# The pace of attention beside the projections: 27 and 26 k steps a head in place of 25, in a hybrid SSD and attention block

## The chip, the core and the metric

The kernel runs on one core of a Trainium2 chip. The core's engines follow streams of their own: TensorE (PE in the profile, its weight loads as PEld), VectorE (DVE), ScalarE (ACT), GpSimd (POOL) and SyncE (SP), which here only issues DMAs. The metric is the time of one execution on the device in microseconds, as the median of several runs.

## The reference, cut to what matters

A block for 512 tokens with 2048 features. One input projection feeds two mixers, a state-space mixer and an attention with three branches; both go through an output projection, and a gated feed-forward follows.

```python
def reference(x, ...):
    u = rmsnorm(x, attn_norm_w)
    z, xbc, dt_raw, q, kc, vc, ks, vs, kw, vw, gate_raw = split(u @ w_in)
    y_ssd = ssd_mixer(z, xbc, dt_raw, ...)
    y_att = nsa_mixer(q, kc, vc, ks, vs, kw, vw, gate_raw, ...)
    h = x + concatenate([y_ssd, y_att]) @ w_out
    v = rmsnorm(h, ffn_norm_w)
    h = h + (silu(v @ w_gate) * (v @ w_up)) @ w_down
    return rmsnorm(h, final_norm_w)

# nsa_mixer: 16 heads of 64, in 4 groups that share keys and values
    p_cmp = softmax(mask(q k_cmp / 8))          # 31 compressed keys
    o_sel = softmax(mask(q_rot ks / 8)) vs      # selected blocks: at 512 tokens all causal ones
    o_win = softmax(mask(q_rot kw / 8)) vw      # a window of 512: again all causal ones
    o = g0 * o_cmp + g1 * o_sel + g2 * o_win
```

## The kernel before, in words

**Number format.** Every large product is done as three matmuls of a high and a low half: high by high, high by low, low by high. ScalarE makes the high half of an operand (`a_hi`, L124), VectorE the low half (`lo`, L127).

**Projection tiles.** The input projection is 41 tiles of 128 output rows (`Unit`), the output projection 16 more. A tile goes through 16 k steps (output tiles 11, 12 or 8); each k step is the three matmuls L234, L235, L236 and then one `sch.tick()`. Weights arrive in sub-tiles of four k steps; `issue_split` forms their halves three sub-tiles ahead (`whi`, `wlo`). After a tile its evacuation runs as a generator (`ev_q`, `ev_ks`, `ev_vs`, `ev_z`, `ev_os`).

**The scheduler in the code.** `Sched` holds generators. A generator emits instructions and then yields a number of ticks to be left alone. `run_until(flags)` ticks, without matmuls of a tile, until the flags are set. `run_unit` (L217) calls it before each tile: L224 asks that the evacuation of the tile two before has ended.

**The tiles beside attention.** In the order they run (L1008 to L1012): Z4, VS1, KS1, Q1a, Q1b, Z5, Z6, Z7, VS2, KS2, Q2a, Q2b, VS3, KS3, Q3a, Q3b, then the 16 output tiles; 256 and 186 k steps. From Z4 on PE's instructions stand in the order in which they are written; the other engines' order is set by the planner of the language. Keys (KS), values (VS) and queries (Q) of group g are made by the tiles that carry its number. Their buffers are two deep: `ev_vs` and `ev_ks` of group g wait, after a few ticks, for the flag ("a", g - 2), set when all of group g - 2 is done (L720, L760). `ev_q` waits in the same way for heads before it.

**Attention.** `attention()` (L811) goes through 112 items: 4 groups, 4 heads, 7 items a head. At step s it emits the scores of item s (`score`: two matmuls, a mask and a minimum on VectorE, the exponential on ScalarE), yields one tick, transposes item s - 3 (`trans`: into one of two banks ps_t, whose halves pth and ptl ScalarE and VectorE read out) and scales item s (`norm`), yields PACE ticks, and for the last item of a branch emits the product with the values (`pvmm`, L919). So a head takes 7 + 18 = 25 ticks. At the start of group g it waits for the keys and the first queries of the group; the first product of a group waits for the values and the compressed branch (`compressed`).

**The join to the feed-forward.** Ahead of the last output tile (8 k steps), `pre_last` (L1054) waits for the end of attention and for the evacuation of the tile before, closes attention's buffers, and opens the feed-forward's in their place. What is left of the output projection (L1231 to L1233) follows the last tile; its weights come from `Z<-in_w_out`, its halves are `R`.

Of the kernel before, what the change touches and what calls it, by code (L numbers as in the profile page):

```python
# [26 lines left out]

NS = [11, 11] + [12] * 13 + [8]
KSUB = 4
PACE = [3, 2, 3, 2, 3, 2, 3]  # L30
LAG = 3
EB = 5
LEAD = 3
# [81 lines left out]
def body(ctx, tc, xT, w_in, w_out, w_gate, w_up, w_down, w1k, w1v, cols, rows, kst, out):  # L115
# [695 lines left out]
    def attention():  # L811
# [48 lines left out]
        def score(g, h, br, i):  # L860
            L = 128 * (i + 1)
            q = R["rq", g, h // 2][:, h % 2, i * 128:(i + 1) * 128]
            p = ps_s()
            o = p[:, 0:L] if i else p[:, 0:256].rearrange("p (b k) -> p b k", b=2)
            for n, t in enumerate(R["k", g]):
                pe.matmul(o, q, t[:, br, 0:L] if i else t[:, :, 0:128], start=(n == 0), stop=(n == 1))
            e = ap.tile([128, 512], F32, tag="e", name="e", bufs=EB)
            m = ap.tile([128, 8], F32, tag="em", name="em", bufs=EB + 1)
            pr[g, h, br, i] = (e, m)
            for b, c, m in sides(br, i, m):  # L870
                dve.tensor_tensor_reduce(e[:, c], p[:, c], kcs(K_AM + 512 - L, L), -0.125, 3e38,
                                         ALU.add, ALU.min, m[:, 0:1])
                act.activation(e[:, c], e[:, c], AF.Exp, scale=-1.0, bias=m[:, 0:1], accum_out=m[:, 1:2])
# [6 lines left out]
        def norm(g, h, br, i):  # L880
            e, m = pr[g, h, br, i]
            for b, c, m in sides(br, i, m):
                gc = (4 * g + h) * 3 + 1 + b
                dve.reciprocal(m[:, 2:3], m[:, 1:2])
                if b:
                    dve.tensor_scalar(e[:, c], e[:, c], m[:, 2:3], gat[:, i, gc:gc + 1],
                                      op0=ALU.mult, op1=ALU.mult)
                else:
                    mul(dve, m[:, 3:4], m[:, 2:3], gat[:, i, gc:gc + 1])
                    a_hi(e[:, c], e[:, c], scale=m[:, 3:4])  # L890

        def trans(g, h, br, i):
            e, m = pr.pop((g, h, br, i))
            if (br, i) in ((0, 1), (2, 0)):
                pt[g, h, br // 2] = (ap.tile([128, 13, 128], F32R, tag="pth", name="pth", bufs=2),
                                     ap.tile([128, 13, 128], F32R, tag="ptl", name="ptl", bufs=2))
            p = ps_t()
            for kb in range(i + 1 if i else 2):
                pe.transpose(p[:, kb * 128:(kb + 1) * 128], e[:, kb * 128:(kb + 1) * 128], ident)
            for b, c, _ in sides(br, i, m):  # L900
                th, tl = pt[g, h, b]
                s = p[:, c].rearrange("p (a b) -> p a b", b=128)
                d = slice(i, 3 * i + i + 1, 3)
                a_hi(th[:, d, :], s)
                lo(dve, tl[:, d, :], s, th[:, d, :])

        def pvmm(g, h, br):
            th, tl = pt.pop((g, h, br))
            if br == 0:
                ch, cl = R["cc", g]  # L910
                o = po[h] = ps_v()
                pe.matmul(o, vpad[:, h, :], ch, start=True, stop=False)
                pe.matmul(o, vpad[:, h, :], cl, start=False, stop=False)
            o = po[h]
            v = R["v", g]
            for kb in range(4):
                for t in (th, tl):
                    rhs = t[:, 4 * kb:3 * kb + 4, :].rearrange("p a b -> p (a b)")
                    pe.matmul(o[:, kb * 128:512], v[:, kb, br, :], rhs, start=False,  # L919
                              stop=(br == 1 and kb == 3 and t is tl))  # L920
            if br == 1:
                if h % 2 == 0:
                    R["at"] = ap.tile([128, 512], F32, tag="at", name="at", bufs=1)
                at = R["at"]
                a, b = (0, 64) if h % 2 == 0 else (64, 0)
                fo = ap.tile([128, 512], F32, tag="fo", name="fo", bufs=1)
                act.activation(fo[a:a + 64, :], o[b:b + 64, :], AF.Copy)
                add(dve, at[a:a + 64, :], o[a:a + 64, :], fo[a:a + 64, :])
                if h % 2:
                    k = 2 * g + h // 2  # L930
                    if "ma" in P2:
                        h_, l_ = P2["ma"][k]
                        a_hi(h_, at)
                        lo(dve, l_, at, h_)
                    else:
                        parts(at_d[k], at)
                        P2["at"] = k
                    sch.flags.add(("at", k))
# [5 lines left out]
        for s in range(n + LAG + 1):  # L944
            if s < n:
                g, h, br, i = items[s]
                if (h, br, i) == (0, 0, 1):
                    yield from sch.wait(("k", g), ("q", g, 0))
                if (h, br, i) == (2, 0, 1):
                    yield from sch.wait(("q", g, 1))  # L950
                if (h, br, i) == (2, 0, 2) and g < 3:
                    sch.add(compressed(g + 1))
                score(*items[s])
                if (br, i) == (1, 3):
                    sch.flags.add(("h", g, h))
            yield 1
            if 0 <= s - LAG < n:
                trans(*items[s - LAG])
            if s < n:
                norm(*items[s])  # L960
            yield PACE[s % len(PACE)]
            if 0 <= s - LAG - 1 < n and items[s - LAG - 1][2:] in ((2, 0), (1, 3)):
                g, h, br, _ = items[s - LAG - 1]
                br %= 2
                if (h, br) == (0, 0):
                    yield from sch.wait(("v", g), ("cc", g))
                pvmm(g, h, br)
                sch.flags.add(("pv", g, h, br))
                if (h, br) == (3, 1):
                    sch.flags.add(("a", g))  # L970
# [652 lines left out]
    def g_rhs(p, lo_):  # L1623
        a = G_POS[V_OF[p]]
        return lambda k: (G[lo_ + k][:, a, 0, :], G[lo_ + k][:, a, 1, :])
# [155 lines left out]
    def down_before(v, n):  # L1781
        def before():
            if n == 1:
                assert v < NJ - 2 or not any(fz.busy[NZ2:])
                add_h(v)
                if v:
                    P2["A2"] = P2["A"][:, 70:76, :]
            elif n == 0 and v == 27:
                x = GRING * 2 + 1
                assert max(i for i, y in enumerate(visits) if y[1] <= x < y[2]) < v  # L1790
                close_pool("t0")
                P2["X"] = open_pool("t0", side="right").tile([128, 32, 128], F32, name="X")
            elif (v, n) == (0, 0):
                close_pool("E")
                P2["E2"] = P2["E"] = open_pool("E").tile([128, NE, 128], F32, name="E2")
        return before
# [13 lines left out]
    for v, (j, a, b) in enumerate(visits):  # L1810
# [14 lines left out]
        for n, p in enumerate(SEQ_D):  # L1825
            blk, sums = q["form"][p]
            if n == 0 and v in (2, 3):
                later[5 + (v == 3)] = len(items)
            s = Step(blk, g_rhs(p, a), bk(p), after=af(p),
                     before=down_before(v, n) if n < 2 else None, sums=sums)  # L1830
# [70 lines left out]
    sch.add(ssd_core())  # L1901
    sch.add(compress())
    sch.add(attention())
    for n, u in enumerate(units[:n_att]):
        if n == 4:
# [97 lines left out]
```

## Time and profile before

| | |
|---|---|
| median of the runs | 2195.72 us (2189.53 to 2196.98, 3 runs) |
| profiled execution | 2193.74 us, span 2192.0 us |
| PE busy | 98% of the span |
| VectorE / ScalarE / GpSimd busy | 81% / 55% / 20% |
| scores of attention, first to last product | 346.8 to 781.5 us |
| last output tile ends | 796.6 us |

The page gives busy time as shares of the span. Where idle time ends at another engine's work, the line names what was waited for, as in `[1.48 <-DVE sc L133]`: idle 1.48 us, ended by VectorE's instruction of line 133 that wrote sc. Matmuls overlap in a pipeline: the duration of one is longer than the distance from its start to the next one's.

### The profile page before, as it was taken

What the parts mean: (1) busy time and instruction counts of PE and PEld (TensorE: products, weight loads), DVE (VectorE), ACT (ScalarE), POOL (GpSimd) and SP (SyncE); (2) the same over time, 40 slices, a digit from 0 to 9 for tenths busy, and PEclk for the clock granted to TensorE, in tenths of its full rate; (3) what the DMA queues carried; (4) which work ended last, traced back from release to release, by engine and by line L of the source; (5) the groups of instructions that cost most, each with busy time, mean ns of one, the idle gap of its engine ahead of it and who ended that gap; (6) DMA issues with size and microseconds to landing.
All of it is one profiled execution on the core that took longest, in us unless ns stands there. A gap on an engine that the chain in (4) does not pass through costs nothing. (4 is left out here: it accounts for less than half of the span.)

```text
span 2192.0 us, 35313 instructions
## 1 busy us (share of the span) xinstructions
PE 2143.6 (98%) x12828; PEld 1891.6 (86%) x12828; DVE 1773.5 (81%) x2799; ACT 1210.5 (55%) x2022; POOL 433.8 (20%) x444
## 2 busy tenths in 40 slices
PE   8999999999999999999999999999999899999997
PEld 6888887888788887888888888888888899999897
DVE  6799767878896658888888888888888888887786
ACT  5465456676676657565555555555555443443353
POOL 0002224424431134000001000000000231222232
PEclk9999999999999999999999999999999999999999
DMA  5222342223464476878888788888878879897973
GB/s 202 92 70 71 127 145 91 72 97 103 144 216 119 108 223 204 252 211 253 229 239 246 218 252 222 245 242 221 254 215 269 292 195 318 239 286 201 320 189 107
DMA packets 179182, 427.17 MB, mean 195 GB/s; under 512 B 20624, under 2 KB 27808, under 8 KB 179008
## 3 DMA queue, kind: packets, MB, share of 16 engines
q1 hardware_dynamic: 139760, 321.66, 43.6%
q0 software_dynamic: 29584, 85.90, 20.1%
q10 hardware_dynamic: 9664, 17.36, 2.2%
q8 instruction: 101, 1.65, 0.3%
q14 instruction: 73, 0.60, 0.1%
HBM read 358.78 MB, written 62.39 MB: 192 GB/s over the span
## 5 line engine op out<-in xcount | busy, mean ns | idle before, releaser
L124 ACT ACTIVATE R<-Z 128x1024 fp32r<-128x1024 f32 (+4 forms) x446 | 406.8, 925 | 395.7 <-DVE Z L136 308.1
L127 DVE TENSOR_TENSOR R<-Z,R 128x1024 fp32r<-128x1024 f32 (+4 forms) x355 | 376.5, 1068 | 39.1 <-issue 13.8
L234 PE MATMUL ps_g<-u,whi 128*128 128x512 f32 x778 | 318.7, 410 | 2.1 <-ACT whi L124 2.1
L236 PE MATMUL ps_g<-u,wlo 128*128 128x512 f32 x778 | 306.7, 394 | 1.0 <-DVE wlo L127 0.8
L235 PE MATMUL ps_g<-u,whi 128*128 128x512 f32 x778 | 305.4, 393 | 0.0
L1227 PE MATMUL ps_s<-u,R 128*128 128x512 f32 (+1 forms) x1160 | 251.5, 347 | 0.6 <-ACT A L1436 0.6
L1227 PEld LDWEIGHTS ps_s<-u,R 128*128 128x128 f32 x1160 | 188.6, 188 | 28.4 <-ACT A L1436 1.2
L127 DVE TENSOR_TENSOR wlo<-wraw,whi 128x512 fp32r<-128x512 f32 x211 | 160.1, 761 | 63.6 <-ACT whi L124 59.9
L124 ACT ACTIVATE whi<-wraw 128x512 fp32r<-128x512 f32 x211 | 131.5, 626 | 112.3 <-PE ps_g L235 80.2
L236 PEld LDWEIGHTS ps_g<-u,wlo 128*128 128x128 f32 x778 | 146.4, 188 | 33.9 <-DVE wlo L127 2.3
L234 PEld LDWEIGHTS ps_g<-u,whi 128*128 128x128 f32 x778 | 146.8, 189 | 24.7 <-ACT whi L124 2.4
L235 PEld LDWEIGHTS ps_g<-u,whi 128*128 128x128 f32 x778 | 147.2, 189 | 22.6
L1227 PE MATMUL ps_t<-u,R 128*128 128x512 f32 (+1 forms) x600 | 131.4, 347 | 0.0
L1227 PE MATMUL ps_g<-u,R 128*128 128x512 f32 x584 | 131.3, 349 | 0.0
L1227 PE MATMUL ps_g<-T,R 128*128 128x512 f32 (+1 forms) x584 | 127.2, 350 | 0.0
L1227 PE MATMUL ps_s<-T,R 128*128 128x512 f32 (+1 forms) x560 | 125.5, 349 | 0.0
L1227 PE MATMUL ps_s<-V,R 128*128 128x512 f32 (+1 forms) x568 | 123.4, 348 | 0.0
L127 DVE TENSOR_TENSOR E<-Z,R 128x1024 fp32r<-128x1024 f32 (+1 forms) x91 | 111.5, 1226 | 4.4 <-PE ps_t L1227 3.8
L136 DVE TENSOR_TENSOR Z<-Z 128x1024 f32<-128x1024 f32 (+4 forms) x99 | 107.1, 1081 | 8.3 <-POOL Z L136 6.4
L1227 PEld LDWEIGHTS ps_t<-u,R 128*128 128x128 f32 x600 | 98.0, 188 | 14.0
L136 DVE TENSOR_TENSOR A<-ps_g,A 128x512 f32<-128x512 f32 (+1 forms) x102 | 67.3, 664 | 51.5 <-PE ps_g L1227 39.1
L1227 PEld LDWEIGHTS ps_g<-u,R 128*128 128x128 f32 x584 | 95.9, 188 | 13.9
(504 smaller groups left out, 5542.8 us busy)
## 6 DMA issues: line engine op xcount, KB each, us to landing
Z<-in_w_up SPq DMA_DIRECT2D x94, 512.0 KB, 4.6
Z<-in_w_gate SPq DMA_DIRECT2D x94, 512.0 KB, 5.5
wraw<-in_w_in SPq DMA_DIRECT2D x164, 256.0 KB, 2.6
g_d<-A SPq DMA_DIRECT2D x147, 256.0 KB, 6.3
Z<-in_w_up POOLq DMA_DIRECT2D x37, 512.0 KB, 7.5
Z<-in_w_gate POOLq DMA_DIRECT2D x37, 512.0 KB, 7.4
u<-g_d SPq DMA_DIRECT2D x70, 256.0 KB, 5.5
Z<-in_w_down SPq DMA_DIRECT2D x55, 320.0 KB, 4.7
```

The source lines that it names most:

```text
L124: act.activation(dst, src, AF.Copy, scale=scale)
L127: eng.tensor_tensor(dst, src, f(hi), ALU.subtract)
L136: eng.tensor_tensor(o, a, b, ALU.add)
L234: pe.matmul(p, hi_t[i][:, j, :], ah, start=(k == 0), stop=False)
L235: pe.matmul(p, hi_t[i][:, j, :], al, start=False, stop=False)
L236: pe.matmul(p, lo_t[i][:, j, :], ah, start=False, stop=(k == u.nk - 1))
L1227: pe.matmul(o, w, x, start=start, stop=(k == n - 1 and o is q), skip_group_check=not fresh[0])
```

## The change

The list of seven PACE values becomes four lists, one for each group. In the first three groups they add up to 20 a head, with the 7 single ticks 27 k steps; in the last group to 19, that is 26.

```diff
-PACE = [3, 2, 3, 2, 3, 2, 3]
+PACE = [[3, 3, 3, 3, 3, 2, 3]] * 3 + [[3, 3, 3, 2, 3, 2, 3]]
...
-            yield PACE[s % len(PACE)]
+            yield PACE[min(s // 28, 3)][s % 7]
```

No instruction is added or removed; they stand at other places among the matmuls of the tiles.

## The prediction

> **What bounds the kernel now.** I read the page's head first, then the windows of the stretch in which attention runs, then the waits of PE alone in it, and last the order of time at the places named. The page says that PE is the engine to follow:
>
> ```profile
> span 2192.0 us, 35313 instructions
> PE 2143.6 (98%) x12828; PEld 1891.6 (86%) x12828; DVE 1773.5 (81%) x2799; ACT 1210.5 (55%) x2022; POOL 433.8 (20%) x444
> ```
>
> All PE work that the change touches stays the same work; it is only dealt out in another order. So the time can move only by PE's idle time and by a lower clock. The windows show where these are. The cut at 584.60 us is the end of the projection tile KS3, the cut at 344.80 the start of Z4 (k step 0 below), and 781.50 is the last matmul of attention. Columns are the window, its length, then PE, PEld, DVE, ACT, POOL busy with counts, the granted clock and DMA.
>
> ```profile
> 344.80:584.60 239.80, 231.25 (x1190) 192.17 (x1189) 196.87 (x508) 166.40 (x381) 87.23 (x93) 0.99 0.30 98
> 584.60:781.50 196.90, 196.57 (x1010) 164.57 (x1009) 138.88 (x389) 125.31 (x301) 47.26 (x58) 1.00 0.50 147
> ```
>
> Of PE's idle time beside attention 239.80 - 231.25 = 8.55 us lie before 584.6, and only 0.33 us after it, at the same pace of 25. The waits of PE in the first window:
>
> ```profile
> PE ps_t L899 <- DVE ptl L127: 3.4, 4, 1.4
> PE ps_g L234 <- ACT whi L124: 2.1, 1, 2.1
> PE ps_t L843 <- DVE sc L133: 1.5, 1, 1.5
> PE ps_g L236 <- DVE wlo L127: 0.8, 2, 0.5
> PE ps_v L919 <- DVE ptl L127: 0.4, 1, 0.4
> ```
>
> They are waits for VectorE and ScalarE: a transpose that finds both ps_t banks unread, a weight half not yet formed. The sum of the rows is 8.2 us.
>
> **Counting the change.** The code deals work by ticks: one k step of a tile (three matmuls, L234 to L236) is one tick, and attention advances by 1 + PACE ticks per score item, seven items a head. I count from k step 0. Attention first waits for the compressed branch until tick 36, six ticks late. The last product of group 1 comes at the end of s = 59, so after 60 items: eight heads of 25 and four items of 4, 3, 4, 3, with the 6 ticks and the one at the start 200 + 14 + 7 = tick 221. The last of group 3 comes after 116 items: 400 + 14 + 7 = tick 421 (k step 420; one tick falls in the gap before the second output tile). The trace agrees: k steps (L235) and score matmuls (L866, two per item) in the same windows are
>
> ```profile
> 344.80:584.60 239.80, 88.46 (x225) 42.84 (x225) 0.99 0.30 98
> 584.60:781.50 196.90, 76.80 (x196) 37.04 (x196) 1.00 0.50 147
> 344.80:584.60 239.80, 30.86 (x122) 21.67 (x122) 0.99 0.30 98
> 584.60:781.50 196.90, 26.04 (x102) 18.14 (x102) 1.00 0.50 147
> ```
>
> 224 to 225 k steps with 61 items, then 196 with 51: 420 and 112. Twenty-two k steps (781.5 to 796.6) then run with no attention beside them.
>
> After the change, the same count gives: the first wait is four ticks, group 1 ends at 8 x 27 + 4 x 4 + 5 = tick 237, group 3 at 12 x 27 + 4 x 26 + 15 + 5 = tick 448. Now the limit at L224: a tile starts only when the tile two before it has been read out and its evacuation has ended. The evacuation of VS3 (ended k step 208) holds at L720 until group 1 is done, because the buffers of v are two. The first q tile of group 3, two tiles after it, starts at k step 224. Before, group 1 was done at 221, three ticks early. After, it is done at 237: the loop of L224 then ticks 13 times **without a matmul of the tile between**. Attention is pushed through these 13 ticks dry, so it catches up: it stands at item 60 at k step 224 (before: item 60 at 221). From there 27 and 26 a head end it at k step 434 instead of 420. That is exactly where the last output tile is opened (L1055), so nothing more is waited for there: 8 k steps run after it in place of 22. So the change has three parts.
>
> *Part 1, k steps 0 to 224: attention slower.* Fewer items share the same stretch, 57 for 61. Nothing is removed. What is gained is at most the idle time there, 8.55 us, and the clock that one of these waits costs:
>
> ```profile
> 370.41 0.63 PE L843 MATMUL ps_t<-ident,sc 128*128 128x128 f32 x4 [1.48 <-DVE sc L133]
> 372.45 0.66 PE L899 MATMUL ps_t<-ident,e 128*128 128x128 f32 x2 [0.73 <-DVE ptl L127]
> 373.34 0.63 PE L235 MATMUL ps_g<-u,whi 128*128 128x512 f32 x1
> 373.77 0.63 PE L236 MATMUL ps_g<-u,wlo 128*128 128x512 f32 x1
> ...
> 783.65 0.39 PE L234 MATMUL ps_g<-u,whi 128*128 128x512 f32 x1
> 783.88 0.39 PE L235 MATMUL ps_g<-u,whi 128*128 128x512 f32 x1
> 784.10 0.39 PE L236 MATMUL ps_g<-u,wlo 128*128 128x512 f32 x1
> 784.33 0.39 PE L234 MATMUL ps_g<-u,whi 128*128 128x512 f32 x1
> ```
>
> ```profile
> 372.00:374.00 2.00, 1.54 (x5) 1.38 (x6) 1.90 (x8) 0.87 (x3) 0.00 (x0) 0.55 0.37 119
> 374.00:376.00 2.00, 2.00 (x6) 1.55 (x6) 0.70 (x2) 1.03 (x2) 0.00 (x0) 0.59 0.03 12
> ```
>
> A k step takes 784.33 - 783.65 = 0.68 us at full clock. At a clock of 0.55 to 0.59 a matmul came every 0.43 us in place of 0.23; over six of them that is 1.2 us. Bounds of the gain: 0 and 8.55 + 1.2 = 9.8 us. The value: a transpose waits for a bank read two items earlier; two items are now 2 x 27/7 k steps apart in place of 2 x 25/7, 0.57 k step or 0.39 us more; three items (the lag from a score to its transpose) are 0.59 us more. The four waits of L899 shorten by 0.39 each (1.56), the one for whi by 0.59, those for wlo and L919 (0.8 and 0.4, shorter than 0.59 each time) go. The one of L843 is left, since its chain counts ticks from the q tile, not items. I take 1.56 + 0.59 + 0.8 + 0.4 = 3.4 us gained.
>
> *Part 2, the 13 dry ticks at k step 224.* They hold 13 x 7/27 = 3.4 items. What an item costs VectorE and ScalarE, from the undisturbed stretch 660 to 781 us with 34 scores:
>
> ```profile
> L127 DVE TENSOR_TENSOR ptl<-ps_t,pth 128x384 fp32r<-128x384 f32 (+3 forms) x39 | 19.1, 490 | 6.2 <-ACT pth L124 5.7
> L871 DVE CUSTOM_DVE_ANT_0 e<-ps_s,kc 128x384 f32<-128x384 f32 (+3 forms) x34 | 16.6, 497 | 14.3 <-PE ps_s L866 14.2
> L886 DVE TENSOR_SCALAR e<-e,em,gat 128x256 f32<-128x256 f32 (+3 forms) x19 | 8.6, 452 | 0.6
> L884 DVE RECIPROCAL em<-em 128x1 f32<-128x1 f32 x35 | 5.7, 163 | 9.1 <-ACT e L873 8.6
> L871 DVE DVE_READ_ACCUMULATOR2_ANT em<- 128x1 f32 x34 | 2.8, 83 | 0.0
> L133 DVE TENSOR_TENSOR em<-em,gat 128x1 f32<-128x1 f32 x16 | 2.5, 157 | 0.4
> ```
>
> That is 55.3 us over 34, 1.63 us of VectorE an item. PE needs, from the second window, (196.57 - 196 x 0.68) / 51 = 1.24 us an item. So in the dry stretch VectorE has 3.4 x 1.63 = 5.5 us to do while PE has 4.2 us, where otherwise each item has 27/7 x 0.68 = 2.6 us of k steps beside it. Idle of PE: at least 0 (what VectorE has left can be done behind the next k steps, whose weight halves are formed three sub-tiles ahead), 1.3 us by these sums, and more by what else stands in VectorE's order at that place, the evacuation of KS3 and the two parts of v:
>
> ```profile
> 585.25 0.68 DVE L133 TENSOR_TENSOR kt<-ps_g,rrow 128x512 f32<-128x512 f32 x1
> 588.06 0.69 DVE L133 TENSOR_TENSOR ro<-kt,kc 128x512 f32<-128x512 f32 x1
> 586.92 0.75 DVE L594 SCALAR_TENSOR_TENSOR lp<-gy,colc,hp 128x512 fp32r<-128x512 f32 x1 [0.98 <-ACT hp L124]
> 583.59 0.42 DVE L127 TENSOR_TENSOR v<-ps_m,v 128x256 fp32r<-128x256 f32 x1
> ```
>
> With all of it (0.68 + 0.69 + 0.75 + 2 x 0.42 = 3.0) the idle is 4.3 us. If it is spread as at 370 us, the clock falls for 1.2 us more: upper bound 5.5 us. I take 2.0 us, near the sum without the evacuations, since KS3's read-out and v are not waited for by an item of the stretch.
>
> The Trainium skill, "TensorE: Matmul & The Clock Gate", section "HAM oscillation", says that the clock halves only after idle gaps beyond about 3.4 us; by that rule 2 us of idle in pieces cost no clock, and a whole dry gap of 4.3 us would cost an estimated 1.7 us of it. The trace differs: 1.48 and 0.73 us of idle within 4 us sufficed at 370 us.
>
> *Part 3, the end.* Groups 2 and 3 run at 27 and 26; with 0.33 us of idle there is nothing to gain. Attention's last matmul now stands 8 k steps (5.5 us) ahead of the first output remainder (L1231) in place of 15.1 us. Before, the order there was:
>
> ```profile
> 777.52 1.91 SPq L1166 DMA_DIRECT2D Z<-in_w_out  x4
> 781.41 0.27 PE L919 MATMUL ps_v<-ptl,v 128*128 128x128 f32 x1
> 784.60 0.69 DVE L127 TENSOR_TENSOR u<-at,u 128x512 fp32r<-128x512 f32 x1 [0.31 <-ACT u L124]
> 786.53 1.90 ACT L124 ACTIVATE R<-Z 128x640 fp32r<-128x640 f32 x3 [0.23 <-issue]
> 788.78 0.69 DVE L127 TENSOR_TENSOR E<-Z,R 128x512 fp32r<-128x512 f32 x1
> 796.57 0.39 PE L1231 MATMUL ps_g<-u,R 128*128 128x512 f32 x1
> ```
>
> The last attention rows u take 785.3 - 781.5 = 3.8 us behind it: within 5.5. The first forms R (1.9 us of ScalarE for three, to 789.5 us with VectorE's) came 8.0 us behind it; if they hang on attention's buffers, they are 8.0 - 5.5 = 2.5 us late. If not, nothing: the loads that feed them were issued from 777.5 us on, ahead of attention's end, so I take 0 and keep 2.5. The DMA issues, on SP's and ScalarE's queues, are the same in number and order.
>
> **Sum.** -3.4 + 2.0 + 0 = -1.4 us. The profiled execution took 2193.74 us, 1.98 below the median 2195.72. So 2192.3 for such an execution and 2194.3 as a median: no change that can be told, since some 0.3% (6.6 us) is what a measurement of this kernel separates from none.
>
> **The rivals.**
> - *The early waits vanish.* All 8.55 + 1.2 us go and the dry stretch costs its 2.0: -7.8, a median of 2187.9. For it: the second window, with fewer items of evacuation, has no wait at all, so the waits may be a threshold. Against: VectorE is busy 196.87 of 239.80 us (82%) there, and 4 items fewer x 1.63 us take 6.5 us of it, 3 points.
> - *The dry stretch decides (slower).* PE runs 13 ticks with nothing to cover VectorE, the evacuations stand in front, the clock falls, and the early waits stay, because they come from the order on VectorE and ScalarE and not from load: +5.5, 2201.2. It decides from the point at which the stretch's idle exceeds the gain of part 1. For it: three parts of idle already tripped the clock once. Against: four items are 4.2 us of PE work.
> - *The end.* The forms are late by 2.5 us: -1.4 + 2.5 = +1.1, 2196.8. Against: the early loads.
> - That the change does nothing is excluded by the counts, except that the dry ticks give most of the slowing back by k step 224.
>
> **How the numbers follow.** The forecast 0.52, the early waits 0.14, the dry stretch 0.22, the end 0.12. The runs of the kernel before went from 2189.53 to 2196.98, so each case has some 4 us about it. Faster by over 0.3%: most of the second case and a little of the first, 0.16. Slower by over 0.3%: two fifths of the dry stretch, which alone is +0.25%, with a little of the end and of the forecast, 0.14. Within: 0.70. The range takes in both outer cases with about 2 us beyond: 2186 to 2203; the forecast's own is 2190 to 2199.
>
> **What would show it.** In the profile after: the number of k steps up to the last L919 of attention is 434 and not 420; between two k steps near 585 us stand some four scores, three sets of transposes and two products with no L234 between; idle of PE there near 2 us; the waits at L899 before it fall from 3.4 us to under 2; no wait at L1231 at the join. It is wrong if the dry stretch is not there, if the early waits stay whole, or if PE waits for forms at the join.

## The result and the profile after

The changed kernel takes 2204.73 us (median of 7 runs, 2201.68 to 2207.55), the kernel before in the same comparison 2195.46 us (7 runs): a ratio of 1.0051, 95% interval 1.0041 to 1.006. It is slower, by 9.3 us between the medians, and 1.7 us above the predicted range. The profiled execution took 2203.51 us. Head of the page after:

```profile
span 2201.7 us, 35334 instructions
PE 2146.3 (97%) x12828; PEld 1894.0 (86%) x12828; DVE 1779.5 (81%) x2799; ACT 1209.4 (55%) x2022; POOL 430.6 (20%) x444
```

The counts of these rows are those of before (the 21 more in all are semaphore instructions), the span is 9.7 us longer. The windows of the kernel after, cut where the predicted pieces meet: k step 0, the stretch without k steps, the end of attention, the end of the last output tile (window, length, PE, PEld, DVE, ACT, POOL busy with counts, clock, DMA):

```profile
344.20:582.00 237.80, 225.73 (x1153) 187.41 (x1152) 194.63 (x479) 158.69 (x358) 86.64 (x94) 0.99 0.31 99
582.00:593.40 11.40, 7.79 (x37) 6.36 (x35) 9.70 (x30) 8.05 (x20) 7.39 (x11) 0.71 0.32 102
593.40:799.60 206.20, 206.20 (x1056) 173.16 (x1055) 140.59 (x391) 127.08 (x308) 41.40 (x51) 1.00 0.50 143
799.60:805.20 5.60, 5.60 (x28) 4.63 (x27) 2.21 (x3) 1.96 (x3) 1.33 (x2) 1.00 0.72 191
```

The same windows for L235 alone (PE and PEld), one matmul for each k step:

```profile
344.20:582.00 237.80, 88.39 (x225) 42.70 (x224) 0.99 0.31 99
582.00:593.40 11.40, 0.00 (x0) 0.00 (x0) 0.71 0.32 102
593.40:799.60 206.20, 82.27 (x210) 39.79 (x210) 1.00 0.50 143
799.60:805.20 5.60, 3.12 (x8) 1.51 (x8) 1.00 0.72 191
```

The first row counts 225, one of which belongs to the tile before and reaches into the window. So the order is the predicted one: 224 k steps, a stretch of 11.4 us without any, then attention to k step 434, then 8. From 593 us to the end of the last output tile PE is not idle. What was lost lies ahead of it: 12.07 us of idle in the first window, where the kernel before had 8.55 in its own, and 3.61 us in the dry stretch, at a clock of 0.71. The same in the windows 340 to 560 and 560 to 812 us, first before, then after:

```profile
340.00:560.00 220.00, 212.05 (x1085) 176.29 (x1084) 176.19 (x447) 151.98 (x344) 85.76 (x90) 0.99 0.28 90
560.00:812.00 252.00, 251.07 (x1268) 209.29 (x1268) 176.18 (x472) 155.91 (x367) 60.93 (x75) 1.00 0.53 160
```

```profile
340.00:560.00 220.00, 207.93 (x1058) 172.32 (x1056) 177.17 (x427) 147.23 (x328) 84.09 (x90) 0.98 0.29 92
560.00:812.00 252.00, 248.39 (x1257) 208.19 (x1257) 175.38 (x482) 154.87 (x373) 57.42 (x70) 0.99 0.50 146
```

Idle goes from 7.95 to 12.07 us in the first and from 0.93 to 3.61 in the second: 6.8 us more. In windows of 4 us, busy time times what the granted clock lacks of 1 adds up to 1.52 us before and 4.55 after: 3.0 us more. Together 9.8 us, the 9.7 of the span. The waits of PE after, 340 to 810 us (total, times, longest):

```profile
PE ps_g L234 <- ACT whi L124: 5.3, 1, 5.3
PE ps_t L899 <- DVE cpl L127: 4.9, 2, 3.2
PE ps_t L843 <- DVE ptl L127: 2.1, 1, 2.1
PE ps_v L919 <- DVE ptl L127: 1.4, 3, 0.7
PE ps_g L236 <- DVE wlo L127: 1.2, 1, 1.2
PE ps_t L899 <- DVE ptl L127: 0.4, 1, 0.4
```

The waits of L899 for ptl fell from 3.4 to 0.4 us, further than forecast. But the one for whi grew from 2.1 to 5.3 at the same k step (200), that of L843 stands at 2.1 where it was 1.5, those of L919 and for wlo add up to 1.4 and 1.2 where they were 0.7 and 0.8, and two for cpl (the low half of the compressed weights, read out of the same two banks) are new, with 3.2 and 1.7.

**The wait for whi.** In this stretch the eight parts of the state-space output are formed beside attention (`ms_parts`, L598 to L606): GpSimd multiplies gy, ScalarE makes hp, VectorE lp. In ScalarE's order three weight halves whi stand directly behind hp of the fourth part. ScalarE, VectorE and GpSimd of the kernel after around it, in order of time (start, duration; idle before and what ended it in brackets):

```profile
549.00 1.09 DVE L133 TENSOR_TENSOR em<-em,gat 128x1 f32<-128x1 f32 x1
...
550.16 1.27 POOL L133 TENSOR_TENSOR gy<-gy,row 128x512 f32<-128x512 f32 x1
...
550.19 0.51 ACT L124 ACTIVATE e<-e,em 128x256 f32<-128x256 f32 x1 [1.42 <-DVE em L133]
...
552.14 0.62 ACT L873 ACTIVATE e<-e,em 128x384 f32<-128x384 f32 x1 [1.16 <-DVE em L871]
...
553.07 1.05 DVE L133 TENSOR_TENSOR em<-em,gat 128x1 f32<-128x1 f32 x1
...
554.22 0.61 ACT L124 ACTIVATE e<-e,em 128x384 f32<-128x384 f32 x1 [1.00 <-DVE em L133]
554.74 0.71 ACT L124 ACTIVATE hp<-gy,colc 128x512 fp32r<-128x512 f32 x1
555.35 1.65 ACT L124 ACTIVATE whi<-wraw 128x512 fp32r<-128x512 f32 x3
```

ScalarE is not short of time: it is idle three times for attention's items (1.42, 1.16, 1.00 us), and the three whi, which then run without waiting for any data, stand behind that. PE's k step stood still for 5.34 us.

**The dry stretch.** PE, then VectorE, then ScalarE there:

```profile
582.41 0.60 PE L843 MATMUL ps_t<-ident,sc 128*128 128x128 f32 x4
582.85 0.49 PE L899 MATMUL ps_t<-ident,e 128*128 128x128 f32 x3
587.05 1.12 PE L899 MATMUL ps_t<-ident,e 128*128 128x128 f32 x4 [3.25 <-DVE cpl L127]
...
583.59 0.75 DVE L594 SCALAR_TENSOR_TENSOR lp<-gy,colc,hp 128x512 fp32r<-128x512 f32 x1 [0.18 <-ACT hp L124]
584.26 0.68 DVE L127 TENSOR_TENSOR wlo<-wraw,whi 128x512 fp32r<-128x512 f32 x1
584.86 0.68 DVE L133 TENSOR_TENSOR ro<-kt,kc 128x512 f32<-128x512 f32 x1
...
586.31 0.69 DVE L127 TENSOR_TENSOR cpl<-ps_t,cph 128x512 fp32r<-128x512 f32 x1
...
582.83 0.73 ACT L124 ACTIVATE hp<-gy,colc 128x512 fp32r<-128x512 f32 x1 [0.91 <-POOL gy L133]
...
584.78 0.60 ACT L124 ACTIVATE cph<-ps_t 128x512 fp32r<-128x512 f32 x1
```

The transposes of the compressed weights (L843) take one of the two banks, so the second L899 waits for cpl. On VectorE cpl stands behind lp, wlo and ro, but it also needs the high half cph, and ScalarE has that only at 585.38, behind hp, which had waited for GpSimd's gy. So VectorE's order alone holds cpl for the last 0.9 us. Behind the 3.25 us the clock was low (the last section tells why the windows are cut here):

```profile
583.41:586.82 3.41, 0.40 (x2) 0.00 (x0) 3.17 (x8) 2.69 (x7) 2.97 (x6) 1.00 0.54 165
586.82:590.23 3.41, 2.82 (x10) 1.95 (x10) 2.88 (x15) 2.87 (x11) 0.98 (x2) 0.50 0.48 162
590.23:593.64 3.41, 3.41 (x14) 3.32 (x15) 2.51 (x7) 1.92 (x4) 2.89 (x4) 0.50 0.03 11
593.64:597.06 3.42, 3.42 (x19) 2.86 (x18) 2.86 (x6) 3.06 (x8) 1.26 (x2) 1.00 0.50 160
```

At the join, the first output remainder follows 5.6 us behind attention without a wait, as forecast:

```profile
805.15 0.39 PE L1231 MATMUL ps_g<-u,R 128*128 128x512 f32 x1
```

### The profile page after: what moved, and what is told of

Read it like the earlier page. It is cut to its first block, busy times and chain, and to the rows that moved or that the text cites. A ratio compares the mean times of both kernels' runs of the same rounds, so it can differ in the third digit from the quotient of the medians.

```text
span 2201.7 us, 35334 instructions
## 1 busy us (share of the span) xinstructions
PE 2146.3 (97%) x12828; PEld 1894.0 (86%) x12828; DVE 1779.5 (81%) x2799; ACT 1209.4 (55%) x2022; POOL 430.6 (20%) x444
## 5 line engine op out<-in xcount | busy, mean ns | idle before, releaser
L124 ACT ACTIVATE R<-Z 128x1024 fp32r<-128x1024 f32 (+4 forms) x446 | 407.0, 925 | 397.6 <-DVE Z L136 303.7
L235 PE MATMUL ps_g<-u,whi 128*128 128x512 f32 x778 | 305.3, 392 | 0.0
L124 ACT ACTIVATE whi<-wraw 128x512 fp32r<-128x512 f32 x211 | 131.2, 625 | 114.9 <-PE ps_g L235 82.5
L235 PEld LDWEIGHTS ps_g<-u,whi 128*128 128x128 f32 x778 | 147.2, 189 | 22.6
L1227 PEld LDWEIGHTS ps_g<-T,R 128*128 128x128 f32 x584 | 96.2, 191 | 13.6
```

Of the source, the lines that this page charges most:

```text
L124: act.activation(dst, src, AF.Copy, scale=scale)
L235: pe.matmul(p, hi_t[i][:, j, :], al, start=False, stop=False)
L1227: pe.matmul(o, w, x, start=start, stop=(k == n - 1 and o is q), skip_group_check=not fresh[0])
```

## The experiments

One table first, since the runs are read by it. Idle is PE's between 340 and 812 us, clock the loss worked out as above, both of the one profiled execution; the sum's distance from before stands beside the ratio of all runs, turned into us with 2193. Pace is given for the groups in order.

| kernel | pace | idle | clock | sum | sum - before | ratio (95%) | in us |
|---|---|---|---|---|---|---|---|
| before | 25 | 8.90 | 1.52 | 10.42 | | | |
| after | 27 27 27 26 | 15.68 | 4.55 | 20.23 | +9.8 | 1.0051 (1.0041, 1.006) | +11.2 |
| e1_lift | 27 27 25 25 | 13.34 | 5.84 | 19.18 | +8.8 | 1.0048 (1.0031, 1.0065) | +10.5 |
| e2_late | 25 25 26 27 | 12.50 | 1.66 | 14.16 | +3.7 | 1.0018 (1.0007, 1.0029) | +3.9 |
| e3_dry | 25 | 11.48 | 2.89 | 14.37 | +4.0 | 1.001 (0.9999, 1.0022) | +2.2 |
| e4_lift26 | 26 26 25 25 | 12.76 | 3.72 | 16.48 | +6.1 | 1.0023 (1.0013, 1.0032) | +5.0 |
| e5_noparts27 | as after | 8.27 | 1.60 | 9.87 | -0.6 | 1.0008 (0.9998, 1.0018) | +1.8 |
| e6_noparts25 | 25 | 4.76 | 1.64 | 6.40 | -4.0 | 0.9963 (0.9948, 0.9978) | -8.1 |
| e9_noparts_lift27 | 27 27 25 25 | 5.28 | 1.72 | 7.00 | -3.4 | 0.9994 (0.9982, 1.0006) | -1.3 |
| e7_rot25 | 25 | 9.22 | 2.89 | 12.11 | +1.7 | 1.000 (0.999, 1.001) | 0.0 |
| e8_fastparts27 | as after | 21.20 | 7.55 | 28.75 | +18.3 | 1.0103 (1.0088, 1.0119) | +22.6 |
| e10_pace24 | 24 24 26 26 | 8.50 | 4.37 | 12.87 | +2.5 | 1.0009 (0.9999, 1.0018) | +2.0 |
| e11_shift5 | 25 | 11.95 | 3.14 | 15.09 | +4.7 | 1.0023 (1.0009, 1.0037) | +5.0 |
| e12_rot27lift | 27 27 25 25 | 7.87 | 6.08 | 13.95 | +3.5 | 1.0016 (1.0007, 1.0026) | +3.5 |
| e13_shift27lift | 27 27 25 25 | 12.72 | 5.82 | 18.54 | +8.1 | 1.0037 (1.0023, 1.005) | +8.1 |
| e14_rot27 | 27 27 27 26 | 8.63 | 5.75 | 14.38 | +4.0 | 1.0022 (1.0011, 1.0034) | +4.8 |
| e16_after_move | as after | 12.60 | 4.47 | 17.07 | +6.7 | 1.0043 (1.0029, 1.0056) | +9.4 |
| e15_rot27lift_move | 27 27 25 25 | 4.72 | 3.17 | 7.89 | -2.5 | 0.9983 (0.9974, 0.9993) | -3.7 |
| e17_before_move | 25 | 10.30 | 1.72 | 12.02 | +1.6 | 1.0005 (0.9995, 1.0015) | +1.1 |

The two columns of differences agree within 2.7 us, except in e6 and e8, where they lie some 4 us apart. So the stretch beside attention carries most of what the kernels differ by, but for e6 (below).

### Is it the dry stretch?

**e1_lift** lets Q3a start while VS3's evacuation still runs, so that the 13 dry ticks go, and goes back to 25 from group 2 on.

```diff
-PACE = [[3, 3, 3, 3, 3, 2, 3]] * 3 + [[3, 3, 3, 2, 3, 2, 3]]
+PACE = [[3, 3, 3, 3, 3, 2, 3], [3, 3, 3, 3, 3, 2, 3], [3, 2, 3, 2, 3, 2, 3], [3, 2, 3, 2, 3, 2, 3]]
...
-            sch.run_until(("evac", n_u - 2))
+            sch.run_until(("evac", n_u - (3 if n_u == 40 else 2)))
```

> 27 k steps a head in groups 0 and 1 as in the change, 25 in groups 2 and 3, and the first q tile of group 3 may start while the evacuation of VS3 still waits, so that no dry ticks fall at k step 224; attention then ends at k step 434, as in the change. Theory A (the loss is the dry stretch, some 3.6 us of idle and 2 to 3 us of half clock, and the longer wait for whi near k step 194, 5.3 in place of 2.1 us, with its clock): the first 224 k steps keep their order, so the long wait stays and the dry stretch goes: some +4 us on the kernel before, 2199.5. Rival B (the slower pace itself costs, wherever the stops fall): +9 us, 2204. Rival C (the wait for whi is a matter of the order the planner gives and need not come back): 0 to -3 us, 2193 to 2195.

Measured: 2202.97 us, near the number of rival B. The 3.25 us wait is gone and the time stays. Behind the same 5.34 us wait for whi the clock now took longer to come back (windows of 4 us):

```profile
556.00:560.00 4.00, 2.78 (x7) 2.03 (x8) 3.32 (x3) 2.58 (x6) 2.44 (x3) 0.50 0.47 137
560.00:564.00 4.00, 4.00 (x15) 3.41 (x14) 2.79 (x7) 1.70 (x4) 0.00 (x0) 0.50 0.77 256
564.00:568.00 4.00, 4.00 (x19) 3.38 (x18) 3.90 (x9) 1.73 (x3) 2.40 (x3) 0.77 0.08 32
```

That is 2.78 x 0.5 + 4 x 0.5 + 4 x 0.23 = 4.3 us of clock, where the kernel after lost 1.75 there; 1.5 us of clock came near 371 us, and 1.4 us of idle between 611 and 650 us. So taking the dry stretch away did not bring the time back: it is not the whole cause.

**e3_dry** is the kernel before with 13 dry ticks at the same place.

```diff
             sch.run_until(("evac", n_u - 2))
+        if n_u == 40:
+            for _ in range(13):
+                sch.tick()
```

> The kernel before (25 throughout), with 13 ticks without a matmul of a tile put in ahead of the first q tile of group 3: the dry stretch by itself. Theory A: it costs some 3.6 us of idle and 2 to 3 us of half clock: +6 us, 2201.5. Rival (the dry stretch costs little by itself, the planner reorders around it, and what the change lost is the slower pace): 0 to +2 us, 2196 to 2197.5.

Measured: ratio 1.001, interval 0.9999 to 1.0022. A wait of 3.46 us stands there, with 1.34 us of clock behind it; 2.96 us more idle than before between 560 and 620 us. The stretch by itself costs 2 to 4 us, and in this kernel the interval only just includes none. PE waits there for ptl and not for cpl, so it is not the same stretch in every item.

**e2_late** keeps 25 in the first two groups and slows the last two.

```diff
-PACE = [[3, 3, 3, 3, 3, 2, 3]] * 3 + [[3, 3, 3, 2, 3, 2, 3]]
+PACE = [[3, 2, 3, 2, 3, 2, 3], [3, 2, 3, 2, 3, 2, 3], [3, 3, 3, 2, 3, 2, 3], [3, 3, 3, 3, 3, 2, 3]]
```

> Only groups 2 and 3 are slowed (25, 25, 26, 27), so attention ends at k step 434 as in the change but without dry ticks at 224. Theory A: no change, 2195.5 within 2 us, since these groups had 0.3 us of idle to give. Rival (the late end of attention delays the join to the feed-forward and what follows, where the change lost 1.4 us): +1.5 to +3 us, 2197 to 2198.5.

Measured: ratio 1.0018. Nothing changes ahead of group 2, and yet 3.3 us of waits come between 560 and 620 us (the longest 2.45, L899 for ptl) and 1.4 behind it, where the kernel before had 0.93 and none: slower by moving the order alone.

**e4_lift26** is e1_lift with 26 in place of 27.

```diff
-PACE = [[3, 3, 3, 3, 3, 2, 3]] * 3 + [[3, 3, 3, 2, 3, 2, 3]]
+PACE = [[3, 3, 3, 2, 3, 2, 3], [3, 3, 3, 2, 3, 2, 3], [3, 2, 3, 2, 3, 2, 3], [3, 2, 3, 2, 3, 2, 3]]
...
-            sch.run_until(("evac", n_u - 2))
+            sch.run_until(("evac", n_u - (3 if n_u == 40 else 2)))
```

> As e1_lift with 26 k steps a head in groups 0 and 1. If the wait for whi near k step 194 grows with the pace (2.1 us at 25, 5.3 at 27): some 3.7 us of it and about +2 us on the kernel before, 2197.5. If it hangs on how the stops of attention fall against the evacuation of the q tile and the parts of the state-space output: any value from 0 to 5 us, not between the two; the time then -2 to +4 us.

Measured: ratio 1.0023; the wait for whi is 6.62 us, longer than at 27 and beyond both expectations: it does not simply grow with the pace.

### Is it the state-space parts?

**e6_noparts25** and **e5_noparts27** are the kernels before and after with the parts' products and halves left out; U is read from gy for both halves.

```diff
-            t = wp.tile([128, 512], F32, tag="raw", name="gy", bufs=4)
-            nc.sync.dma_start(t, gy_d[k])
-            mul(pool, t, t, P2["row2"])
...
-            parts(gp_d[k], t, col(C_SN + k))
...
-            nc.sync.dma_start(f(U[:, :, k, :]), gp_d[k].rearrange("s p t -> p s t"))
+            [nc.sync.dma_start(f(U[:, i, k, :]), gy_d[k]) for i in range(2)]
```

> The changed kernel without the work of ms_parts (the state-space output's rows are not scaled and not split into halves; the output projection reads the raw rows for both halves, so its numbers differ): no load of gy, no product on GpSimd, no hp and lp, no stores. Theory D (the growth of the wait for whi near k step 194 hangs on these parts, whose hp stands ahead of three whi in ScalarE's order and waits for GpSimd): that wait is gone, under 0.5 us, and this kernel lies some 4 us or less above the same cut of the kernel before (its dry stretch, which the forced one put at +2 to +4 us). Theory B (a slower pace costs by itself): the wait stays and the two cut kernels differ by 9 us or more.

> The kernel before with the same cut of ms_parts. Both theories: faster than the kernel before, since VectorE, ScalarE and GpSimd lose 8 x 0.75, 8 x 0.72 and 8 x 1.3 us beside attention. Theory D: the wait of 2.1 us for whi goes and some more, 3 to 5 us faster, 2189 to 2191. If PE's idle time there is independent of the parts: within 1 us of the kernel before.

Measured: 0.9963 at 25 and 1.0008 at 27. The wait for whi is gone in both, as expected. But 2194.44 and 2183.99 us lie 10.4 us apart, where theory D had 4 or less and theory B 9 or more: without the parts 27 loses about as much against 25 as with them (9.3). So the parts are not what the whole loss hangs on. Idle and clock up to 812 us show 3.5 us of the 10.4. The first product of the output remainder (L1231) starts at 790.0 us at 25 and at 794.9 at 27, so half of the difference comes behind it; why is open. At 25 the waits that are left lie all ahead of 500 us:

```profile
PE ps_t L899 <- DVE ptl L127: 3.0, 3, 1.5
PE ps_t L843 <- DVE sc L133: 1.4, 1, 1.4
```

**e9_noparts_lift27** is e1_lift with the same cut.

> e1_lift (27, 27, 25, 25, no dry ticks at k step 224) with the cut of ms_parts: the raw rows are read in place of the scaled and split ones. Here only the pace of groups 0 and 1 differs from e6_noparts25, no parts and no dry stretch. If pace alone neither gains nor loses (the waits at the start of attention and of the head ends stay as long): within 2.5 us of e6_noparts25, that is 2184 to 2187. If the slower pace costs by itself (theory B): like e5_noparts27, 2193 to 2195.

Measured: 0.9994. Idle is 5.28 us against 4.76 at 25: without the parts this list of pauses at 27 gains nothing either. The medians of e6 and e9 lie 5.7 us apart, where 2.5 or less were expected if the pace alone did nothing. Idle and clock up to 812 us explain 0.6 of it; L1231 starts at 792.6 us, 2.6 behind e6. The rest stays open.

**e8_fastparts27** packs the parts closer in the kernel after (`yield 3` for `yield 8`).

> The changed kernel with ms_parts paced at 5 ticks a part in place of 10, so that all eight parts are done by k step 189, before the evacuation of Q2b. Theory D: the wait for whi near k step 194 is gone; what is left of the loss is the dry stretch, +2 to +4 us on the kernel before, unless the denser parts make waits of their own near k steps 150 to 189. Theory B: the loss stays, +9 us.

Measured: 1.0103, where the loss was expected to shrink or stay. Waits for whi and wlo come to 13 us. Packing the parts closer doubles the loss.

### Or the place of the stops?

**e7_rot25** keeps 25 and moves the short pauses: `PACE = [3, 3, 2, 3, 2, 3, 2]`. **e10_pace24** runs faster, 24 in the first two groups. **e11_shift5** keeps all pauses and forms all parts 5 ticks later (`yield 13 if k == 0 else 8`).

> 25 k steps a head as before, with the seven values of PACE turned by one (3, 3, 2, 3, 2, 3, 2), so that every stop of attention moves by a k step or less. If the waits hang on how the stops fall (theory D): the waits for whi and ptl before k step 224 change by a few us either way with the pace unchanged, -4 to +5 us. If they hang on the pace (theory B): the same 8 to 9 us of idle, within 1.5 us of the kernel before.

> 24 k steps a head in groups 0 and 1, 26 in groups 2 and 3, no dry ticks. If less room for an item made longer waits (the reasoning by which the change was to gain): the early waits grow, from 8.5 to some 11 us or more, +2 to +4 us. If the waits hang on how the stops fall and not on the pace: between -3 and +5 us with other waits than at 25.

> The kernel before, pace 25, with all eight parts of the state-space output 5 ticks later. If the waits near k step 194 hang on where the parts fall against the evacuation of Q2b: the wait for whi of 2.1 us goes or grows by more than 1 us, the time by -4 to +5 us. If it belongs to Q2b and attention alone: 2.1 us again and no change.

Measured: 1.000, 1.0009 and 1.0023. The wait for whi is gone in all three, and in all three others came: 1.71, 1.80 and 1.50 us in e7; 3.46 us at the first L843 in e10; 2.33 and 2.12 us for ptl in e11.

Then the same at 27. **e12_rot27lift** is e1_lift, **e14_rot27** the kernel after, with the short pause of a head at another place (in e14 those of the last group too; its edit is shown); **e13_shift27lift** is e1_lift with the parts 5 ticks later.

```diff
-PACE = [[3, 3, 3, 3, 3, 2, 3]] * 3 + [[3, 3, 3, 2, 3, 2, 3]]
+PACE = [[3, 3, 2, 3, 3, 3, 3]] * 3 + [[3, 2, 3, 3, 2, 3, 3]]
```

> The kernel with the dry ticks lifted (27 k steps a head in groups 0 and 1, then 25; 2203.0 us, ratio 1.0048), with the pauses of a head in another order: 3, 3, 2, 3, 3, 3, 3. The pace stays 27; only the place of the short pause moves, so some stops of attention stand one k step elsewhere. Alignment theory: what costs is where the stops fall against the evacuations and the state-space parts, so the 5.3 us wait for whi and the clock it costs change by several us and the ratio lands anywhere from 1.000 to 1.010, by several tenths of a percent away from 1.0048 (2194 to 2200 if the wait goes). Pace theory: 27 itself costs, by its longer overlap with the parts and by pushing attention's end to k step 434; then the waits add up to the same 15 to 18 us of idle and clock and the time stays 2201 to 2205.

> The kernel with the dry ticks lifted (27, 27, 25, 25; 2203.0 us), with all eight state-space parts formed 5 ticks later. Alignment theory: the 5.3 us wait for whi near k step 194 goes, and with it some 4 us of low clock behind it; other waits of 1 to 2.5 us come, as they did when the same was done at 25; the time falls to 2194 to 2199. Pace theory: waits of the same sum come elsewhere, 2201 to 2205.

> The changed kernel, dry ticks and all, with the pauses in another order: 3, 3, 2, 3, 3, 3, 3 in the first three groups and 3, 2, 3, 3, 2, 3, 3 in the last. Alignment theory: the whi wait changes by several us, the dry stretch keeps its 3 to 6 us, the time is 2197 to 2202 or, with a worse alignment, above 2207. Pace theory: 2203 to 2206, as the changed kernel.

Measured: 1.0016, 1.0037, 1.0022. At the same pace, with the dry ticks (e14) and without (e12), 6 to 7 us of the 11 are gone by moving the short pauses. In e14 the dry stretch costs 2.23 us of idle and no clock. So more than half of the loss hangs on where the stops stand and not on how many ticks a head takes. The wait for whi is 3.75 us in both, with some 4.3 us of clock behind it. In e13 it is 1.3, but waits for wlo of 4.2 us in all came, and the time lies between the two expectations.

**e15_rot27lift_move**, **e16_after_move** and **e17_before_move** move one part alone, the fourth, by 5 ticks, in e12, in the kernel after and in the kernel before.

```diff
-            yield 8
+            yield (8, 8, 8, 13, 3, 8, 8, 8)[k]
```

> The changed kernel with one of the eight state-space parts, the fourth, formed 5 ticks later (its pause 13, the next one's 3, so that the others stay). On ScalarE two of the three weight halves whi then stand in the written order ahead of the exponentials and of hp, where in the changed kernel all three stood behind hp. Theory: the 5.34 us wait for whi near k step 194 hangs on that place alone; it goes, the dry stretch stays at 3 to 6 us of idle and clock, and the time falls by 3 to 6 us, to 2197 to 2200 beside a before of 2193 (ratio 1.002 to 1.0035). Rival: another wait of the same size takes its place, ratio 1.0045 or more.

> The kernel at 27, 27, 25, 25 with the dry ticks lifted and the pauses in the order 3, 3, 2, 3, 3, 3, 3 (ratio 1.0016), with the fourth state-space part formed 5 ticks later. There the wait for whi was 3.75 us and the clock lost behind it 4.3 us. Theory: both go, idle and clock together come to 6 to 8 us between 340 and 812 us where the kernel before had 10.4, and the time is 2 to 5 us under the kernel before (ratio 0.998 to 0.999). Rival: other waits come, ratio 1.0005 to 1.002.

> The kernel before (25 throughout) with the fourth state-space part formed 5 ticks later. Its wait for whi was 2.1 us, with no clock lost behind it in the profiled run. Theory: the wait goes, some of it comes back as other waits, ratio 0.998 to 1.000. Rival: as when all parts were 5 ticks later, the waits that come are longer, ratio 1.001 to 1.003.

Measured: 1.0043, 0.9983, 1.0005. In each the wait for whi at k step 200 is gone. In e17, which ended between its two expectations, 2.7 us for ptl came further on. In e15 one of 1.8 us for wlo came, at k step 212. Its waits of PE between 340 and 812 us, and its windows:

```profile
PE ps_t L843 <- DVE ptl L127: 2.1, 1, 2.1
PE ps_g L236 <- DVE wlo L127: 1.8, 1, 1.8
PE ps_v L919 <- DVE ptl L127: 0.5, 1, 0.5
```

```profile
340.00:560.00 220.00, 217.27 (x1115) 182.08 (x1113) 175.74 (x446) 151.30 (x341) 86.78 (x92) 0.99 0.29 95
560.00:812.00 252.00, 250.02 (x1255) 208.39 (x1255) 179.09 (x479) 160.25 (x377) 63.33 (x77) 0.99 0.54 161
```

Its early idle is 2.73 us against 7.95 before, and with 2189.55 us (2192.98 for the kernel before beside it) it is faster than the kernel before by 0.07 to 0.26%, and so than both kernels of the comparison: 27 in the first two groups need not cost. In e16 the expectation was missed: nothing is left of the 5.34 us at k step 200, but these waits came further on:

```profile
565.74 0.50 PE L234 MATMUL ps_g<-u,whi 128*128 128x512 f32 x1 [1.31 <-ACT whi L124]
568.12 0.50 PE L236 MATMUL ps_g<-u,wlo 128*128 128x512 f32 x1 [1.65 <-DVE wlo L127]
575.56 0.51 PE L234 MATMUL ps_g<-u,whi 128*128 128x512 f32 x1 [0.60 <-ACT whi L124]
```

The dry stretch still has 2.6 us of idle and 3.0 of clock behind it. So the largest single wait could be taken out of the changed kernel, and some 2 us of 11 came back. Own buffers for hp, lp and gy, which would free the parts from the weights' four, weren't tried.

## Why the prediction was wrong

**The counts** were right to the k step: group 1 at tick 237, 13 dry ticks, about four scores, three sets of transposes and two products in them, attention's end at k step 434.

**Part 1 failed, and with it the forecast.** It gave each wait the added room of its items (0.39 or 0.59 us) and summed 3.4 us of gain. The step that failed is "I take 1.56 + 0.59 + 0.8 + 0.4 = 3.4 us gained". For the first term more came than forecast: L899 for ptl went from 3.4 to 0.4 us. The other three went the other way: whi, to shrink by 0.59, grew from 2.1 to 5.3; wlo and L919, to go, stand at 1.2 and 1.0. And the sum has no term for new waits (1.7 for cpl). These waits hang not on the room of an item but on which instruction stands ahead of which on ScalarE, VectorE and PE, and moving the stops changes that. Early idle rose by 4.1 us in place of falling by 3.4. The bounds, 0 to 9.8 of gain, left out a loss altogether. That early idle hangs on the places is shown by e12, e14 and e15: at the same 27 it was 6.3, 6.3 and 2.7 us with other places, and 12.1 with those of the change. What the room is worth by itself is not shown: e15 also moves a part, the same move at 25 (e17) has 5.1 us, and without the parts 27 had more idle than 25.

**Part 2** had the mechanism right and the size wrong: 2.0 us forecast, 5.5 as upper bound; 3.6 us of idle and 2.8 of clock, 6.4 together, were measured. The step that failed is "near the sum without the evacuations, since KS3's read-out and v are not waited for by an item of the stretch". No item waits for their data, but cpl stands behind kt, lp, wlo and ro on VectorE, and cph behind hp on ScalarE. The transposes L843 of the compressed branch, which hold one of the two banks, were not in the working at all; and the 1.2 us of clock were taken from a dip of half the length. In e3 and e14 the stretch cost 2 to 4 us, so the forecast value is at the low end of what such a stretch takes.

**Part 3** held: no wait at L1231 up to the join. Between 812 and 880 us, where the feed-forward begins, the kernel after has 1.1 us more of idle than before (3.82 and 2.74); e15, whose pauses add up to those of e1, has 2.40, so a late end alone does not make it.

**The rivals.** "The dry stretch decides" gave the right sign and 2201.2 us. The sentence in it that the early waits come from the order on VectorE and ScalarE and not from load was the right one. That its number came near is luck: it let the early waits stay, and with the stretch lifted the time was still 2203. No rival let the early waits grow, which is where the largest part went, and the range ended 1.7 us short for that.

**What stays open.** Why a dip of the clock lasts two steps behind one wait and three behind another (below), and so some 3 us between runs of similar order; why 27 costs 10.4 us against 25 without the parts (e5 and e6), half of it behind attention; and how a good place of the stops could be told ahead, without the trace of it.

## What to carry to other kernels

Where a hand-written interleave feeds several in-order engines, a change of its pace is first of all a change of places: the existing waits that it shortens are one side of the sum, and a term for new waits, as large as those that such shifts show in the kernel, belongs on the other. Look in the trace for instructions with early data standing behind ones with late data (here weight halves behind a state-space part and attention's exponentials), move that one instruction and the pauses, and keep the pace for last. Take the ticks at which a coded limit such as L224 binds from a count before and after; that part of the forecast was exact.

## What the runs showed of the hardware

**The clock's dips do not follow the idle time alone, but stand on a grid.** In e17 the waits at 370 us were those of the kernel before, 1.47 and 0.73 us, and cost no clock; in the kernel before they did. After a wait of 2.11 us for whi the kernel before lost nothing and e3 1.5 us; after the same 5.34 us, 1.75 us were lost in one kernel and 4.3 in another. The clock in the traces shows what differs. In all 19, every spell of half clock except the one that runs over the end lasts 3.41 us or two or three times that, and within one execution the spells start whole multiples of 3.413 us apart: in the kernel before at 372.21, 856.90, 1717.06 and 2065.22 us, in the kernel after at 552.68 and 586.82. From one execution to the next the grid lies elsewhere. Windows on these grids, the kernel before and then e17:

```profile
368.80:372.21 3.41, 1.45 (x9) 0.88 (x7) 3.28 (x10) 2.21 (x7) 0.00 (x0) 1.00 0.39 116
372.21:375.62 3.41, 3.17 (x9) 2.62 (x10) 2.40 (x8) 1.90 (x5) 0.00 (x0) 0.50 0.23 77
```

```profile
367.87:371.28 3.41, 1.94 (x12) 1.58 (x11) 2.92 (x9) 2.73 (x9) 0.56 (x1) 1.00 0.67 209
371.28:374.69 3.41, 2.68 (x14) 1.93 (x13) 3.22 (x10) 2.23 (x6) 0.00 (x0) 1.00 0.23 77
```

In the kernel before both waits reach into one step, with 1.96 us of idle, and the next step runs at half clock; in e17 the grid parts them, 1.47 and 0.73 us, and none follows. Between 340 and 812 us of the 19 traces, each of the 29 steps at full clock with 1.9 us or more of PE idle was followed by one at half clock; of those with less than 1.6 us one was (1.11 us, in e10). The two losses behind 5.34 us come out the same way: in the kernel after the dip began at 552.68 and spent 3.34 of its 6.83 us inside the wait, (6.83 - 3.34) / 2 = 1.75; in e1 it began at 555.61, lasted 10.24 us and spent 1.61 of them there, (10.24 - 1.61) / 2 = 4.3. So a part of what such a wait costs is where the grid happens to fall. Why one dip had two steps and the other three is not shown. The Trainium skill, "TensorE: Matmul & The Clock Gate", section "HAM oscillation", names idle gaps of more than about 3.4 us as what throttles; here some 2 us of idle within a step sufficed, so the measurement decides.

**A tiny VectorE instruction beside GpSimd.** The product em of 128x1 elements takes 157 ns in the mean (16 of them, in the prediction's rows); in the rows above it took 1.09 and 1.05 us while GpSimd instructions of 1.28 and 1.26 us ran (548.79 to 550.07 and 552.85 to 554.11 us, each ending with it to 0.02 us), and a scaling of e by em on ScalarE (L124) waited for it each time. The Trainium skill, "SBUF — State Buffer", section "Who interferes with whom", says that a VectorE instruction with two inputs in SBUF contends with a GpSimd instruction that reads SBUF; the trace agrees with its 1.09 us in place of 0.157. How much of the wait for whi comes from it was not tested by itself: e5, e6 and e9 took away GpSimd's gy and ScalarE's hp together.
